# The MLP's second product by one level of Strassen's algorithm, a quarter of the 4096 features at a time, with tokens as rows, then turned back

## The chip, the cores and the metric

The kernel runs on one core of a Trainium2 chip. The core has five engines that work side by side, each through its own queue in order: TensorE (PE in the rows; its weight loads are shown apart as PEld), VectorE (DVE), ScalarE (ACT), GpSimd (POOL) and SyncE (SP), which issues the DMA transfers. They wait for each other through semaphores. SBUF is the on-chip memory of 128 partitions, PSUM the memory that TensorE writes its results to. The metric is the device time of one execution in microseconds (us), the median of three.

## The reference, cut to what matters

Two layers over 512 tokens of 1024 values each. The token mixers (attention, an RWKV-7 scan, a short convolution) stay as they are. The change is about the last line of a layer:

```python
for l in range(2):
    ...                                       # mixers, gates, x = x + merged @ w_out[l]
    h2 = rms_norm(x, mlp_norm[l])             # (1, 512, 1024)
    x = x + jnp.square(jax.nn.relu(h2 @ w_up[l])) @ w_down[l]   # up: 1024x4096, down: 4096x1024
```

`rms_norm(x, g) = x * rsqrt(mean(x*x) + 1e-6) * g`, a factor for each token and a gain for each of the 1024 values.

## The kernel before

**Number format.** All is float32, and every product is made as three TensorE products of a shorter type (`F32R`). Each operand is split into an upper part `hi` (the value cast to `F32R`) and a lower part `lo` (value minus `hi`). A product is then `hi*hi + hi*lo + lo*hi`: the three `mm` of `gemm_steps` (L283, L285, L287). A weight block of 128x512 is loaded to a `raw` tile by SyncE (L245), ScalarE casts it to `hi` (L246), VectorE subtracts for `lo` (L247); there are 4 buffers for `raw` and 4 for `hi` and `lo`. `split` and `split_into` do the same for activations.

**Layout.** The residual `xt` (tile `am`) has features on partitions: 8 tiles of 128 features x 512 tokens. An output tile of a product, 128 features x 512 tokens, is one bank of PSUM; it takes 8 blocks of 128 input features times 3, so 24 matmuls of 128x512, with the weights as the stationary operand and the activations moving.

**The MLP** (L1232 to L1259) goes through the 4096 inner features in four quarters `q`. In a quarter, 8 tiles of the first product are made from `h2`; ScalarE rectifies each out of PSUM (L1245), VectorE multiplies it by its PSUM tile, which squares it (L1246), and `split_into` makes the parts `us`. Then come 8 tiles of the second product, of 8 blocks of `us` each; VectorE multiplies each by the norm's factor (L1254, `rstd2`, the square of the token's factor spread over 128 partitions) and adds it to the residual (L1256). In the fourth quarter each tile goes out by DMA (L1259), in layer 0 to `x_spill`, in layer 1 to the output. PSUM tiles take turns over the tags g, a, b, c with two buffers each.

The norm's gain is in `h2` (`norm_in`). Its factor is not: `norm_scale` squares `xt` on ScalarE (L363) and sums over tiles on VectorE (L368); TensorE sums over partitions; the factor per token is then spread over all partitions by `spread`:

```python
pb = pt(pst)
for b in range(NB):
    e = tl("tok", (P, 4, C)).rearrange("p a b -> p (a b)")[:, 0:P]
    V.tensor_copy(e, rs[:, b:b + 1].to_broadcast([P, P]))
    nc.tensor.transpose(pb[:, b * P:(b + 1) * P], e, ident)
A.copy(dst, pb)
```

**What sets the order.** TensorE's instructions stand in the order in which the program is written. Those of the other engines are put in order at build time by the scheduler of the tile framework, by its own estimates of when operands are ready; a DMA is issued in that order too. A tile of a tag waits until the reader of the buffer's last content is done.

## Time and profile before

| | |
|---|---|
| median of 3 runs | 1600.34 us (1600.29 to 1600.41) |
| profiled execution, whole time | 1599.76 us |
| its span (first to last instruction) | 1598.0 us |
| TensorE busy | 1586.9 us |
| VectorE busy | 1026.8 us |
| ScalarE busy | 662.8 us |
| granted clock of TensorE | 1.00 |

"Busy" is the time in which an engine has an instruction under way. Neighbouring matmuls overlap, so the time of one is read from the distance of two starts. A row of the timeline gives start, duration, engine, line, operation, what is written from what is read, and how many equal ones are merged; in square brackets stands how long the engine was idle before, and what ended that.

### The profile page before, as it was taken

To read this page: it belongs to the slowest core of one execution; us is meant where nothing else is said; L and a number is where in the kernel's file an instruction comes from. 1 tells how busy PE (TensorE), PEld (TensorE's weight loads), DVE (VectorE), ACT (ScalarE), POOL (GpSimd) and SP (SyncE) were. 2 spreads that over 40 slices of the span, in tenths; PEclk is the share of its full clock that TensorE was granted. 3 is DMA by queue.
4 is the path that set the end of the run, shared out by engine and by line. 5 is a ranking of instruction groups with operands and counts; after the bars stand their busy time and mean duration, and the time that the engine had idled before them with its cause. 6 is when DMAs were issued, how large, how long until landed. Compare 5 with 4: busy or idle time off the path is not lost.

```text
span 1598.0 us, 22465 instructions
## 1 busy us (share of the span) xinstructions
PE 1586.9 (99%) x8046; PEld 1292.3 (81%) x8046; DVE 1026.8 (64%) x2035; ACT 662.8 (41%) x1470; POOL 184.9 (12%) x192
## 2 busy tenths in 40 slices
PE   9999999999999999999999999999999999999998
PEld 7888778877888888888877887888778888888887
DVE  8889677687654454444568986686886554444453
ACT  5433565454443332324334334655544423333241
POOL 1312015112000000000022221241130000000000
PEclk9999999999999999999999999999999999999999
DMA  5323322214323333333433242222143333333332
GB/s 178 106 70 119 107 61 80 76 54 163 102 93 98 96 98 99 94 98 99 140 91 86 86 132 90 61 73 73 54 165 106 93 93 99 99 94 98 99 94 97
DMA packets 84639, 156.25 MB, mean 98 GB/s; under 512 B 10032, under 2 KB 12080, under 8 KB 84016
## 3 DMA queue, kind: packets, MB, share of 16 engines
q1 hardware_dynamic: 84528, 154.83, 32.0%
q8 instruction: 63, 1.03, 0.3%
q14 instruction: 48, 0.39, 0.1%
HBM read 145.87 MB, written 8.91 MB: 97 GB/s over the span
## 4 chain that ended last, share of the span: by engine, by line
PE 98%; DVE 1%; DMA 0%; ACT 0%; issue 0%; SPq 0%; DVEq 0%
PE pg L283 16%; PE pg L285 16%; PE pg L287 16%; PE pb L283 4%; PE pb L287 4%; PE pb L285 4%; PE pa L287 4%; PE pc L287 4%; PE pc L283 4%; PE pa L283 4%; PE pa L285 4%; PE pc L285 4%; PE pa L1160 2%; PE pc L1186 1%; PE pb L1174 1%; PE pa L968 1%
## 5 line engine op out<-in xcount | busy, mean ns | idle before, releaser
L246 ACT CAST hi<-raw 128x512 fp32r<-128x512 f32 (+1 forms) x494 | 304.0, 618 | 592.2 <-PE pg L285 243.7
L247 DVE TENSOR_TENSOR lo<-raw,hi 128x512 fp32r<-128x512 f32 (+1 forms) x494 | 358.7, 727 | 239.9 <-ACT hi L246 235.0
L285 PE MATMUL pg<-xg,hi 128*128 128x512 f32 x736 | 296.8, 403 | 0.0
L283 PE MATMUL pg<-xg,hi 128*128 128x512 f32 x736 | 295.2, 401 | 0.7 <-DVE z L600 0.7
L287 PE MATMUL pg<-xg,lo 128*128 128x512 f32 x736 | 290.7, 395 | 0.0
L283 PEld LDWEIGHTS pg<-xg,hi 128*128 128x128 f32 x736 | 138.3, 188 | 33.5 <-issue 3.0
L287 PEld LDWEIGHTS pg<-xg,lo 128*128 128x128 f32 x736 | 138.4, 188 | 31.2 <-issue 3.4
L285 PEld LDWEIGHTS pg<-xg,hi 128*128 128x128 f32 x736 | 138.4, 188 | 30.8 <-issue 3.4
L330 POOL TENSOR_TENSOR t<-t,mhalf 128x4 f32<-128x4 f32 (+1 forms) x26 | 46.7, 1797 | 563.2 <-DVE t L341 535.0
L283 PE MATMUL pb<-xg,hi 128*128 128x512 f32 x144 | 56.4, 392 | 0.0
L287 PE MATMUL pb<-xg,lo 128*128 128x512 f32 x144 | 56.1, 389 | 0.0
L285 PE MATMUL pb<-xg,hi 128*128 128x512 f32 x144 | 56.1, 389 | 0.0
L1164 ACT ACTIVATE inv<-pa,t 128x128 f32<-128x128 f32 (+3 forms) x64 | 33.7, 527 | 47.7 <-DVE t L1162 44.9
L283 PE MATMUL pg<-mix,hi 128*128 128x512 f32 x128 | 51.4, 402 | 0.0
L287 PE MATMUL pg<-mix,lo 128*128 128x512 f32 x128 | 50.2, 393 | 0.0
L287 PE MATMUL pa<-xg,lo 128*128 128x512 f32 x128 | 50.0, 391 | 0.0
L283 PE MATMUL pc<-xg,hi 128*128 128x512 f32 x128 | 50.0, 390 | 0.0
L285 PE MATMUL pa<-xg,hi 128*128 128x512 f32 x128 | 49.8, 389 | 0.0
L287 PE MATMUL pc<-xg,lo 128*128 128x512 f32 x128 | 49.8, 389 | 0.0
L283 PE MATMUL pa<-xg,hi 128*128 128x512 f32 x128 | 49.8, 389 | 0.0
L285 PE MATMUL pc<-xg,hi 128*128 128x512 f32 x128 | 49.8, 389 | 0.0
L285 PE MATMUL pg<-mix,hi 128*128 128x512 f32 x112 | 44.5, 397 | 0.0
(453 smaller groups left out, 3353.4 us busy)
## 6 DMA issues: line engine op xcount, KB each, us to landing
raw<-in_w_dram SPq DMA_DIRECT2D x492, 256.0 KB, 2.6
z_spill<-z SPq DMA_DIRECT2D x16, 256.0 KB, 3.2
inv<-z_spill SPq DMA_DIRECT2D x16, 256.0 KB, 5.5
raw<-in_wq_dram SPq DMA_DIRECT2D x12, 192.0 KB, 2.4
am<-in_x_dram SPq DMA_DIRECT2D x8, 256.0 KB, 4.9
raw<-in_wkv_dram SPq DMA_DIRECT2D x8, 256.0 KB, 2.6
am<-in_x_dram SPq DMA_DIRECT2D x2, 1024.0 KB, 6.3
x_spill<-am SPq DMA_DIRECT2D x8, 256.0 KB, 2.8
```

Of the source, the lines that this page charges most:

```text
L246: A.copy(hi[:, c], raw[:, c])
L247: V.tensor_tensor(out=lo[:, c], in0=raw[:, c], in1=hi[:, c], op=ALU.subtract)
L283: mm(dst, hi[:, c0:c0 + P], ah, start=(k == 0), stop=False)
L285: mm(dst, hi[:, c0:c0 + P], al, start=False, stop=False)
L287: mm(dst, lo[:, c0:c0 + P], ah, start=False, stop=(k == n - 1))
L330: G.tensor_tensor(out=y, in0=v, in1=mhalf.to_broadcast([P, n]), op=ALU.pow)
L968: mm(pu[rr, hs], Zf[h // 2][rr, (h % 2) * 4 + b], R_[rr, hs], start=True, stop=True)
L1160: mm(psc[:, 0:n], qT[hf][h // 2][0:HD, h % 2, b * P:n], kT[hf][h // 2][0:HD, h % 2, 0:n], start=True, stop=True)
L1164: A.activation(out=pe[:, 0:n], in_=psc[:, 0:n], func=AF.Exp, bias=nm[:, h:h + 1], accum_out=rsum[:, h:h + 1])
L1174: nc.tensor.transpose(pq[:, kb * P:(kb + 1) * P], pe[:, kb * P:(kb + 1) * P], ident)
L1186: mm(po[halves[i], f], Vm[hf][kb // 2][:, kb % 2, 2 * f + i], pT[2 * f + i][:, kb * P:(kb + 1) * P], start=(kb == 0), stop=(kb == b))
```

## The change

The second product of a quarter, 512 tokens x 1024 features times 1024 features x 1024 outputs, is cut into halves along all three: A11, A12, A21, A22 are 256 tokens x 512 features, the weights' quarters 512 features x 512 outputs. One level of Strassen's algorithm (Winograd's form) makes it from 7 products of the halves instead of 8, with sums of activations (`S1` to `S4`) and of weights before them and sums of the results behind them. Each of the 7 is 2 token tiles of 128 tokens x 512 outputs, each of 4 blocks times 3, so 24 matmuls of 128x512. Activations are the stationary operand now and weights the moving one, so the results have tokens on partitions ("token-major").

- The sums of activations (L1311 to L1315 of the changed kernel) are made on VectorE on halves of 256 columns; the square is ScalarE's.
- Of the 16 weight blocks of a quarter, 12 are loaded during the first product into tiles that the mixers used before (`room`: `wa`, `wb`, `wc`, `wd`) and stay there; the last four are loaded into `wd` while S3 runs. The sums of weights are VectorE subtractions in place (L1324, L1325, and `less`, L1359). `split_block` makes `hi` and `lo` of each block as it is needed; the 4 buffers of `hi` and `lo` are the ones that the first product uses.
- A product's PSUM tiles (`px` with tag g, `pz` with a, `yp` with b) go on from one product to the next, and are added into the token-major sums `ya` (tag `mg`) by `add_out`, times the token's factor `r2` as a scalar per partition. The first product has tag c for itself, two buffers.
- In the last quarter `finish` turns 4 tiles of 128x128 back on TensorE, adds them to the residual and sends this part out, in rows of 512 bytes.
- `spread` is no longer called for this norm. For layer 1 the eight feature tiles of `xt` are used in the order 4 to 7, 0 to 3 (`K_ORDER`).

```diff
+K_ORDER = [tuple(range(KD)), (4, 5, 6, 7, 0, 1, 2, 3)]
+UP_ORDER = (0, 4, 1, 5, 2, 6, 3, 7)
+DOWN_ORDER = ((0, 0), (0, 1), (1, 1), (1, 0))
...
+    def split_block(src):
+        hi = tl("hi", (P, WW), F32R, bufs=BUFS["hl"])
+        lo = tl("lo", (P, WW), F32R, bufs=BUFS["hl"])
+        A.copy(hi, src)
+        V.tensor_tensor(out=lo, in0=src, in1=hi, op=ALU.subtract)
+        return hi, lo
...
-        rstd2, h2_steps, h2_spread = norm_scale(xt, True)
+        h2_steps, h2_at = norm_scale(xt, pst="a")
...
+        ya = [[tl("mg") for _ in range(2)] for _ in range(NB)]
+        room = [tl("col", (P, T + 1))[:, 0:T] for _ in range(7)] + [tl("kql", (P, 520))[:, 0:T] for _ in range(4)]
+        room += [tl("ext", (P, T + 1), bufs=1)[:, 0:T], tl("z"), tl("z"), tl("rstd", bufs=1), tl("mg")]
+        wa, wb, wc, wd = (room[4 * i:4 * i + 4] for i in range(4))
+        yp = [pt("b") for _ in range(2)]
...
+        def add_out(pd, b, dh):
+            r_ = r2[:, b:b + 1]
+            if (b, dh) in seen:
+                V.scalar_tensor_tensor(out=ya[b][dh], in0=pd, scalar=r_, in1=ya[b][dh], op0=ALU.mult, op1=ALU.add)
+            else:
+                A.activation(out=ya[b][dh], in_=pd, func=AF.Copy, scale=r_)
+            seen.add((b, dh))
+
+        def finish(b, dh):
+            pf = pt("c", (P, 4, P))
+            for i in range(4):
+                nc.tensor.transpose(pf[:, i], ya[b][dh][:, i * P:(i + 1) * P], ident)
+            part = xt[:, 4 * dh:4 * dh + 4, b * P:(b + 1) * P]
+            V.tensor_tensor(out=part, in0=pf, in1=part, op=ALU.add)
+            dst = xd if l < NL - 1 else out
+            nc.sync.dma_start(out=dst.rearrange("p (k t) -> p k t", t=T)[:, 4 * dh:4 * dh + 4, b * P:(b + 1) * P], in_=part)
+
         for q in range(4):
...
+            for n_, m in enumerate(UP_ORDER):
+                pu = pt("c")
+                run(gemm_steps(pu, None, h2), h2_steps if (q, n_) == (0, 1) else None)
...
                 rl = tl("inv")
                 A.activation(out=rl, in_=pu, func=AF.Relu)
-                V.tensor_tensor(out=rl, in0=pu, in1=rl, op=ALU.mult)
-                us.append(places(m, "mg") if q % 2 else places(m, None))
-                split_into(us[m], rl)
-            for m in range(8):
-                pd = pt(ptags[pi % 4])
-                pi += 1
-                gemm(pd, None, us)
-                d_ = tl("inv")
-                V.tensor_tensor(out=d_, in0=pd, in1=rstd2, op=ALU.mult)
-                xm = xt[:, m]
-                V.tensor_tensor(out=xm, in0=xm, in1=d_, op=ALU.add)
-                if q == 3:
-                    dst = xd if l < NL - 1 else out
-                    nc.sync.dma_start(out=dst[:, m * T:(m + 1) * T], in_=xm)
+                A.activation(out=rl, in_=rl, func=AF.Square)
+                us[m] = rl
+                if m >= 4:
+                    j = m - 4
+                    ua, ub = us.pop(j), us.pop(m)
+                    split_into(act["A11", j], ua[:, H1])
+                    s12, s34 = tl("inv"), tl("inv")
+                    V.tensor_tensor(out=s12[:, H1], in0=ua[:, H2], in1=ub[:, H2], op=ALU.add)
+                    V.tensor_tensor(out=s12[:, H2], in0=s12[:, H1], in1=ua[:, H1], op=ALU.subtract)
+                    split_into(act["S1S2", j], s12)
+                    V.tensor_tensor(out=s34[:, H1], in0=ua[:, H1], in1=ua[:, H2], op=ALU.subtract)
+                    V.tensor_tensor(out=s34[:, H2], in0=ub[:, H1], in1=s12[:, H2], op=ALU.subtract)
+                    split_into(act["S3S4", j], s34)
+                    split_into(act["A12A22", j], ub)
+
+                if n_ < 6:
+                    for i in (2 * n_, 2 * n_ + 1):
+                        down_block(i, (wa + wb + wc)[i])
+                elif n_ == 6:
+                    for j in range(4):
+                        V.tensor_tensor(out=wd[j], in0=wc[j], in1=wb[j], op=ALU.subtract)
+                        V.tensor_tensor(out=wb[j], in0=wb[j], in1=wa[j], op=ALU.subtract)
...
+            px, pz = [pt("g") for _ in range(2)], [pt("a") for _ in range(2)]
+            def product(a, blocks, acc, start, outs, before=None, after=None, by_tokens=False):
+                ws = {}
+                for t, j in [(t, j) for t in range(2) for j in range(4)] if by_tokens else \
+                        [(t, j) for j in range(4) for t in range(2)]:
+                    if j not in ws:
+                        if before:
+                            before(j)
+                        ws[j] = split_block(blocks[j])
+                        if after:
+                            after(j)
...
+                    mm(acc[t], ah[:, c], hi, start=(start and j == 0), stop=False, skip_group_check=True)
+                    mm(acc[t], ah[:, c], lo, start=False, stop=False, skip_group_check=True)
+                    mm(acc[t], al[:, c], hi, start=False, stop=(j == 3), skip_group_check=True)
...
+            product("A11", wa, px, True, [(0, 0)])
+            product("S1", wb, pz, True, [(1, 1)])
+            product("S2", wb, px, False, [(0, 1)], before=less(wb, wc, wb))
+            product("S3", wd, px, False, [(1, 1)], after=lambda j: down_block(12 + j, wd[j]))
+            product("S4", wc, pz, False, [(0, 1)])
+            if last:
+                finish(2, 1)
+                finish(3, 1)
+            product("A12", wd, yp, q == 0, [(0, 0)] if last else [])
+            if last:
+                finish(0, 1)
+                finish(1, 1)
+            product("A22", wb, px, False, [(1, 0)], before=less(wb, wd, wb), by_tokens=last)
+        finish(2, 0)
+        finish(3, 0)
```

In this place on TensorE the program goes from the last block of S2 to the first of S3, in the second quarter of layer 0. `pg_6116` and `pg_6117` are `px[0]` and `px[1]`; `hi` and `lo` are parts of a weight block, `ar` and `mix` of activations.

```order
L1344 MATMUL pg_6116<-hi_6238,ar_4975 128x512
L1345 MATMUL pg_6116<-lo_6239,ar_4975 128x512
L1346 MATMUL pg_6116<-hi_6238,ar_4975 128x512
L1344 MATMUL pg_6117<-hi_6238,ar_4975 128x512
L1345 MATMUL pg_6117<-lo_6239,ar_4975 128x512
L1346 MATMUL pg_6117<-hi_6238,ar_4975 128x512
L1344 MATMUL pg_6116<-hi_6250,mix_4958 128x512
L1345 MATMUL pg_6116<-lo_6251,mix_4958 128x512
```

The first matmul of S3 writes the tile that S2 has just finished, so `add_out` has to read it out in between; before, a product of 24 matmuls had the other buffer of its tag, and then three more tags, to go on in.

This is VectorE's queue at the same place: L248 makes the lower part of a block of weights, L1359 and `col`, `kql`, `ext`, `z` are blocks of weights and their differences, L1277 is `add_out`.

```order
L1359 TENSOR_TENSOR kql_4994<-ext_4998,kql_4994 128x512
L1277 SCALAR_TENSOR_TENSOR mg_4984<-pa_6118,r_0_5149,mg_4984 128x512
L1277 SCALAR_TENSOR_TENSOR mg_4986<-pa_6119,r_0_5149,mg_4986 128x512
L248 TENSOR_TENSOR lo_6228<-col_4993,hi_6227 128x512
L248 TENSOR_TENSOR lo_6239<-kql_4994,hi_6238 128x512
L248 TENSOR_TENSOR lo_6251<-z_4999,hi_6250 128x512
L248 TENSOR_TENSOR lo_6262<-z_5000,hi_6261 128x512
L1277 SCALAR_TENSOR_TENSOR mg_4980<-pg_6116,r_0_5149,mg_4980 128x512
L248 TENSOR_TENSOR lo_6273<-rstd_5001,hi_6272 128x512
L1277 SCALAR_TENSOR_TENSOR mg_4982<-pg_6117,r_0_5149,mg_4982 128x512
L1359 TENSOR_TENSOR col_4991<-z_4999,col_4991 128x512
L248 TENSOR_TENSOR lo_6284<-mg_5002,hi_6283 128x512
```

The two additions from `px` stand with one lower part between them, behind four lower parts of S2 and S3; from the first sum of activations of the last up tile (L1311) to the second of these additions there are 28 rows in VectorE's queue.

And this is VectorE at the end of layer 0, before and then after; L311 and L326 are the norm's lower parts for layer 1, L247 and L262 lower parts of loaded weights, L368 and L384 sums of squares, L1288 adds turned tiles to the residual.

```order
L1254 TENSOR_TENSOR inv_7665<-pc_7628,rstd_4955 128x512
L247 TENSOR_TENSOR lo_7792<-raw_7790,hi_7791 128x512
L1256 TENSOR_TENSOR am_4586<-am_4586,inv_7665 128x512
L368 TENSOR_TENSOR inv_7705<-inv_7701,inv_7703 128x512
L368 TENSOR_TENSOR inv_7709<-inv_7705,inv_7707 128x512
L311 SCALAR_TENSOR_TENSOR xg_7698<-am_4586,pp_82,xg_7697 128x512
```

```order
L1277 SCALAR_TENSOR_TENSOR mg_4983<-pg_7524,r_0_5149,mg_4983 128x512
L1288 TENSOR_TENSOR am_4586<-pc_7849,am_4586 128x4x128
L326 SCALAR_TENSOR_TENSOR xg_7891<-am_4586,pp_82,xg_7890 128x512
L1288 TENSOR_TENSOR am_4586<-pc_7856,am_4586 128x4x128
L384 TENSOR_TENSOR inv_7927<-inv_7923,inv_7925 128x512
L326 SCALAR_TENSOR_TENSOR xg_7895<-am_4586,pp_82,xg_7894 128x512
L262 TENSOR_TENSOR lo_7959<-raw_7957,hi_7958 128x512
L384 TENSOR_TENSOR inv_7931<-inv_7927,inv_7929 128x512
L1277 SCALAR_TENSOR_TENSOR mg_4985<-pg_7525,r_0_5149,mg_4985 128x512
```

Between the last two additions from `px`, on which the last two calls of `finish` wait, seven other operations stand now.

## Rows read from the trace of the kernel before

**Rows 1.** The page of the profile: the span, the engines' busy time, TensorE's granted clock in 40 slices (tenths of full speed), and the shares of the chain of work that ended last, by engine.

```profile
span 1598.0 us, 22465 instructions
PE 1586.9 (99%) x8046; PEld 1292.3 (81%) x8046; DVE 1026.8 (64%) x2035; ACT 662.8 (41%) x1470; POOL 184.9 (12%) x192
...
PEclk9999999999999999999999999999999999999999
...
PE 98%; DVE 1%; DMA 0%; ACT 0%; issue 0%; SPq 0%; DVEq 0%
```

**Rows 2.** Busy time of each engine in three stretches of the MLP of layer 0; behind the engines the granted clock, the DMA engines' share and GB/s.

```profile
508.00:549.00 41.00, 41.00 (x182) 33.97 (x181) 18.90 (x29) 10.61 (x18) 0.00 (x0) 1.00 0.33 98
549.00:590.00 41.00, 41.00 (x182) 33.95 (x181) 20.65 (x31) 17.36 (x30) 0.00 (x0) 1.00 0.35 99
590.00:631.00 41.00, 41.00 (x182) 33.95 (x182) 19.00 (x30) 9.58 (x17) 0.00 (x0) 1.00 0.33 97
```

**Rows 3.** The timeline of TensorE in the MLP of layer 0: the first matmul of one tile and the first of the next, with 23 left out between.

```profile
472.42 0.39 PE L283 MATMUL pg<-xg,hi 128*128 128x512 f32 x1
...
477.86 0.39 PE L283 MATMUL pa<-xg,hi 128*128 128x512 f32 x1
```

**Rows 4.** The timeline of TensorE where `spread` stands in the MLP of layer 0 (L350), and the two matmuls behind it.

```profile
466.05 0.38 PE L350 MATMUL pc<-ident,tok 128*128 128x128 f32 x2
466.64 0.47 PE L350 MATMUL pc<-ident,tok 128*128 128x128 f32 x2 [0.21 <-DVE tok L349]
466.87 0.47 PE L283 MATMUL pc<-xg,hi 128*128 128x512 f32 x1
467.18 0.39 PE L285 MATMUL pc<-xg,hi 128*128 128x512 f32 x1
```

**Rows 5.** The timeline of TensorE in the attention part: four transposes of 128x128, merged, and the two matmuls behind them.

```profile
374.04 0.60 PE L1174 MATMUL pb<-ident,inv 128*128 128x128 f32 x4
374.39 0.48 PE L285 MATMUL pg<-xg,hi 128*128 128x512 f32 x1
374.71 0.39 PE L287 MATMUL pg<-xg,lo 128*128 128x512 f32 x1
```

**Rows 6.** The timeline of TensorE in the attention part: first and last of 8 matmuls with weights as the stationary operand, then first and last of 21 with activations as the stationary operand.

```profile
212.96 0.40 PE L285 MATMUL pg<-xg,hi 128*128 128x512 f32 x1
...
214.58 0.39 PE L287 MATMUL pg<-xg,lo 128*128 128x512 f32 x1
...
218.19 0.39 PE L1053 MATMUL pa<-prep,prep 128*128 128x512 f32 x1
...
222.84 0.40 PE L1055 MATMUL pb<-prep,col 128*128 128x512 f32 x1
```

**Rows 7.** Groups of instructions by line and form: count, busy time, mean ns of one, idle time before. The first two are of the stretch 467 to 816 us, the others of the whole span (VectorE's, then ScalarE's).

```profile
L247 DVE TENSOR_TENSOR lo<-raw,hi 128x512 fp32r<-128x512 f32 x129 | 89.0, 690 | 96.8 <-ACT hi L246 95.3
L246 ACT CAST hi<-raw 128x512 fp32r<-128x512 f32 x128 | 79.5, 621 | 190.5 <-PE pc L285 47.2 <-PE pa L285 44.5 <-PE pg L285 44.0
...
L1229 DVE SCALAR_TENSOR_TENSOR am<-pg,am 128x512 f32<-128x512 f32 x16 | 11.1, 692 | 23.8 <-PE pg L287 23.8
...
L911 DVE TENSOR_TENSOR yb<-yb,t 128x256 f32<-128x256 f32 x8 | 3.4, 420 | 0.1
...
L363 ACT ACTIVATE inv<-am 128x512 f32<-128x512 f32 x32 | 19.0, 619 | 0.0
```

**Rows 8.** The timeline of VectorE: three operations in a row of which none reads what another wrote.

```profile
829.53 0.68 DVE L545 TENSOR_TENSOR col<-pa,rstd 128x512 f32<-128x512 f32 x1
830.13 0.68 DVE L545 TENSOR_TENSOR col<-pb,rstd 128x512 f32<-128x512 f32 x1
830.73 0.68 DVE L545 TENSOR_TENSOR col<-pg,rstd 128x512 f32<-128x512 f32 x1
```

**Rows 9.** The timeline of ScalarE: a cast of weights and the rectification behind it.

```profile
548.59 0.62 ACT L246 CAST hi<-raw 128x512 fp32r<-128x512 f32 x1 [2.10 <-PE pa L285]
549.12 0.59 ACT L1245 ACTIVATE inv<-pa 128x512 f32<-128x512 f32 x1
```

**Rows 10.** The timeline of all engines at the kernel's end, from the last matmul to the last store.

```profile
1592.98 0.39 PE L287 MATMUL pc<-mg,lo 128*128 128x512 f32 x1
1593.41 0.69 DVE L1254 TENSOR_TENSOR inv<-pc,rstd 128x512 f32<-128x512 f32 x1 [4.02 <-PE pc L287]
1594.13 0.69 DVE L1256 TENSOR_TENSOR am<-am,inv 128x512 f32<-128x512 f32 x1
1594.85 0.33 SPq L1259 DMA_DIRECT2D out_dram<-am  x1
```

**Rows 11.** Transfers, from four views: a step of the chain that ended last (from the reader that frees the buffer to the first use), two rows of the issues by line (count, KB each, median us to landing), SyncE's own queue at 377 us, and the engines, clock, DMA share and GB/s from 380 to 390 us.

```profile
192.52 2.76 DMA raw<-in_wkv_dram
...
raw<-in_w_dram SPq DMA_DIRECT2D x492, 256.0 KB, 2.6
...
inv<-z_spill SPq DMA_DIRECT2D x16, 256.0 KB, 5.5
...
377.67 0.33 SPq L245 DMA_DIRECT2D raw<-in_w_dram  x1
378.04 2.33 SPq L1213 DMA_DIRECT2D inv<-z_spill  x5
...
380.00:390.00 10.00, 10.00 (x68) 8.17 (x67) 5.17 (x11) 3.99 (x8) 3.31 (x3) 1.00 0.89 318
```

More of the change, by code (lines that the diff above doesn't have):

```diff
@@ L351, in spread, with norm_in, norm_scale @@
         A.copy(dst, pb)
-    def norm_in(xt, gcol):
-        return [split("xg", xt[:, k], gcol[:, k:k + 1]) for k in range(KD)]
-    def norm_scale(xt, squared, behind=None):
+    def norm_in(xt, gcol, order=range(KD)):
+        parts = {k: split("xg", xt[:, k], gcol[:, k:k + 1]) for k in order}
+        return [parts[k] for k in range(KD)]
+    def norm_scale(xt, behind=None, order=range(KD), pst="c"):
         acc = None
-        for k in range(KD):
+        for k in order:
             s = tl("inv")
@@ new lines, in trunk @@
+        places_ = [tl("mix", (P, T), F32R) for _ in range(8)] + [tl("prep", (P, T), F32R) for _ in range(10)]
+        for _ in range(4):
+            both = tl("ar", (P, 2, T), F32R)
+            places_ += [both[:, 0], both[:, 1]]
+        places_ += [tl("mg", (P, T), F32R) for _ in range(2)]
+        H1, H2 = slice(0, 256), slice(256, T)
+        act = {}
+        for j in range(4):
+            p_ = places_[7 * j:7 * j + 7]
+            act["A11", j] = (p_[0][:, H1], p_[0][:, H2])
+            for i, (n1, n2) in enumerate((("S1", "S2"), ("S3", "S4"), ("A12", "A22"))):
+                h_, l_ = p_[1 + 2 * i], p_[2 + 2 * i]
+                act[n1, j], act[n2, j] = (h_[:, H1], l_[:, H1]), (h_[:, H2], l_[:, H2])
+                act[n1 + n2, j] = (h_, l_)
@@ new lines, in trunk, with down_block @@
+        ya = [[tl("mg") for _ in range(2)] for _ in range(NB)]
[3 more added lines that the diff above has]
+        yp = [pt("b") for _ in range(2)]
+        seen = set()
+        def down_block(i, dst):
+            n = sum(sizes[:first + 16 + i]) * P
+            nc.sync.dma_start(out=dst, in_=w[n:n + WW * P].rearrange("(p n) -> p n", p=P))
@@ new lines, in product @@
+            def product(a, blocks, acc, start, outs, before=None, after=None, by_tokens=False):
[8 more added lines that the diff above has]
+                            after(j)
+                    hi, lo = ws[j]
+                    ah, al = act[a, j]
+                    c = slice(t * P, (t + 1) * P)
+                    mm(acc[t], ah[:, c], hi, start=(start and j == 0), stop=False, skip_group_check=True)
+                    mm(acc[t], ah[:, c], lo, start=False, stop=False, skip_group_check=True)
+                    mm(acc[t], al[:, c], hi, start=False, stop=(j == 3), skip_group_check=True)
+                    if by_tokens and j == 3:
+                        for th, dh in outs:
+                            add_out(acc[t], 2 * th + t, dh)
+                        if t == 0:
+                            finish(0, 0)
+                            finish(1, 0)
+                if not by_tokens:
+                    for t in range(2):
+                        for th, dh in outs:
+                            add_out(acc[t], 2 * th + t, dh)
@@ new lines, in less @@
+            def less(dst, a_, b_):
+                return lambda j: V.tensor_tensor(out=dst[j], in0=a_[j], in1=b_[j], op=ALU.subtract)
+            last = q == 3
+            product("A11", wa, px, True, [(0, 0)])
[6 more added lines that the diff above has]
+                finish(3, 1)
```

53 lines of the change are left out of this document (24 added, 29 removed).

## The prediction

> **What bounds the kernel now.** I read the page first: TensorE is busy for 1586.9 of 1598.0 us, VectorE 64%, ScalarE 41%; the clock row reads 9 in every slice, and the chain that ended last is 98% TensorE [rows 1]. A kernel with such a page gets faster only by what leaves TensorE's queue, as long as nothing that is put on the other engines makes TensorE wait. The table by stages says the same of the two MLPs: 41.00 of 41.00 us busy, VectorE near 19 to 21 us of 41, ScalarE 10 to 17, clock 1.00 [rows 2]. Next I took the price of a product from its pace, not from its "busy" of 0.39 us, since neighbours overlap: 24 matmuls of 128x512 start between 472.42 and 477.86, so one costs 0.2267 us and an output tile of 24 costs 5.44 us [rows 3].
>
> **What leaves TensorE.** Before, a quarter of the second product is 8 tiles of 24, so 192 matmuls; after, it is 7 products of 24, so 168. That is 24 fewer in each of 4 quarters of 2 layers: 192 x 0.2267 = **43.5 us less**. The spread of the norm's factor over all rows goes too (the factor now rides as a scalar per token): in its place in the trace the next matmul starts at 466.87 instead of 466.05, and the one after 0.31 us later instead of 0.23 [rows 4], so 0.9 us a layer, **1.8 us less**.
>
> **What comes to TensorE.** Sixteen calls of `finish`, four 128x128 transposes each. Four transposes of this kind stand at 374.04; the matmul behind starts 0.35 later, and the next one 0.32 after that instead of 0.23 [rows 5], so four cost 0.44 us and the sixteen **7.0 us more**. The Trainium skill (TensorE: Matmul & The Clock Gate, Part 4: PE-mode transpose) gives about 275 ns for a single 128x128 transpose inside a kernel. By it the 64 would cost 17.6 us and the sum below would be 10.6 us worse; the trace has four in 0.44 and does not agree.
>
> The products have the same shape but other roles: activations stationary, weights moving. The nearest row is a product of this form in the attention part: 20 starts from 218.19 to 222.84, 0.2325 us each; its neighbours in the old roles run 7 starts from 212.96 to 214.58, 0.2314 each [rows 6]. So most of the slower pace belongs to that stretch, and 0.0011 to the roles. Bounds for 1344 such matmuls: 0 and 1344 x 0.0058 = 7.8 us; I take 1344 x 0.0011 = **1.5 us**, since [rows 3] are of the MLP and it is the quieter stretch.
>
> **What VectorE and ScalarE get.** In the first half of a quarter (8 tiles, 43.5 us) and the second (168 matmuls, 38.1 us), an operation of 512 columns takes 0.69 us on VectorE and 0.62 on ScalarE, a multiply-add out of PSUM 0.69, 256 columns 0.42 [rows 7]. VectorE starts one that does not depend on the last 0.60 us after it, not 0.69 [rows 8], and ScalarE 0.53 [rows 9]. Second half on VectorE: 28 lower parts of weights, 8 differences, 12 additions into `ya`: 48 x 0.605 = 29.0 of 38.1 us. First half: 16 lower parts, 12 of activations, 8 differences, 20 pieces of 256 columns at 0.335 (0.42 less the same overlap): 28.5 of 43.5 us. ScalarE has 28 x 0.53 = 15 us in the second half, and less than 30 in the first; its square is a function that the kernel runs already, at 0.62 [rows 7]. Neither is the bound on average, so what counts is a place where VectorE's queue is late.
>
> **The late place.** Take t = 0 where product A11 starts. ScalarE casts the last block of it, then rectifies (0.53 later) and squares (0.63 later) the last up tile, 0.62 us, so VectorE can begin on that tile at t = 1.8. From there 28 rows stand without a pause in its order, L1311 to the second addition from `px`: 4 of 256 columns, 24 of 512. TensorE wants:
> - the lower part of S1's fourth block at 5.44 + 3 x 1.36 + 0.23 = 9.75. Fourteen rows stand ahead (4 x 0.335 + 10 x 0.605 = 7.4), so it starts at 9.2 and is there at 9.9: 0.15 late;
> - S2's third at 14.0; 21 rows ahead, there at 14.15: 0.15 late;
> - `px[0]` read out when S3 begins, 16.3 + 0.3: its addition starts when S2's last matmul into it is through (16.3 - 4 x 0.23 + 0.3 late + 0.43 to see it [rows 10] = 16.1) and is done by 16.85: 0.25 late;
> - `px[1]` 0.68 later: its addition is two rows on, done at 18.1: 0.55 late.
>
> That is 1.1 us for a quarter. The first quarter of a layer has none of it (its first sums go to ScalarE by copies); I leave 0.2. At the end of layer 0 the last addition from `px` stands behind eight more rows, of which seven belong to norms, splits and turned tiles: started when the first token tile is done they take about 8 x 0.62 = 5.0, then 0.7 for the addition, against 4.0 us of TensorE's second tile and three calls of `finish`: 1.8 late. In layer 1 nothing stands between: 0.5 (0.43 to see the last matmul, 0.69, less the third `finish`, 0.44, and what overlaps). Waits: 6 x 1.1 + 2 x 0.2 + 1.8 + 0.5 = **9.3 us more**.
>
> **Loads.** The kept blocks (`wd`, then `wc`, `wb`) are loaded into their places when their last split has read them, and VectorE's order has subtractions that wait for these loads (L1359 after S3's blocks). From the end of a reader to the first use of a loaded block the chain has 2.76 us; the median of the weight loads is 2.6 [rows 11]. With 2.76 the three subtractions of S3 wait 0.2, 0.3 and 0.9 us on VectorE and the blocks behind still come in time: 0. SyncE issues one in 0.33 to 0.47 us [rows 11], and some eight in eleven us are 2 MB, 190 GB/s; the trace has carried 318 [rows 11].
>
> **The tail.** Before: 1592.98 (last matmul) to 1598.0, 5.0 us, with two VectorE operations and the store [rows 10]. After: the wait and the four transposes are counted above; behind them stand 0.2 us of transposes still running, one VectorE operation and the same store of 3.1 us, 4.1 us after TensorE's last slot against 4.8 before: **0.7 us less**. Its rows of 512 instead of 2048 bytes I price between 0 and 1 us and take 0.
>
> **The sum**, against the profiled execution of 1599.8 us (1598.0 and 1.8 around it): -43.5 - 1.8 + 7.0 + 1.5 + 9.3 - 0.7 = -28.2, so 1571.6. The median of the runs shown lies 0.6 above that execution, so I forecast **1572 us**, 1.8% less. With the low bounds (pace 0, waits of half the size) it is 1566, with the high one for the pace 1578.
>
> **Rivals.**
> 1. VectorE has no overlap in this mix. [rows 8] speaks against it; for it, that 28 operations with waits on three other engines are not the three starts shown there. With 0.69 and 0.42 a step, the 28 rows end at 1.8 + 4 x 0.42 + 24 x 0.69 = 20.0 instead of 17.7, so 3.4 us late a quarter instead of 1.1; six quarters give 14 us more: **1586**. The Trainium skill (VectorE: DVE Perf Modes, The DRAIN you can't avoid) says that an operation starts only when the one before has left the pipe; that is this rival, and the trace, where starts lie 0.60 apart at 0.69 each [rows 8], does not agree.
> 2. Slower than before: the loads land late, and VectorE waits in order for them. In the burst of reloads at 378 the median landing is 5.5 us [rows 11]. The loads in S3 hang one behind the other (split, load, subtraction, split), so each us past about 3 costs about 2 us a quarter: at 5.5 it is 5 more in eight quarters, 38 us: 1610. It breaks even where a quarter waits 4.6 us, at a landing of 5 us. Against it: that burst was eight loads in five us with the DMA engines at 0.89; here four stand in five to six us.
> 3. The pace of [rows 6] is that of the roles: 6.3 us more, **1578**.
> 4. Nothing of VectorE's queue shows, and the pace is that of [rows 3]: 1562.
>
> **Chances.** The forecast with waits of 5 to 16 us (1566 to 1579) 0.58; rival 1 and other ways to lose 10 to 20 us in VectorE's queue (1580 to 1592) 0.2; rival 3 0.08; rival 4 (below 1566) 0.06; rival 2 0.08, of which 0.05 slower, 0.02 about even and 0.01 still faster. From 0.2% (3.2 us) on the runs, which lie within 0.12 us, tell a change. So faster 0.93, same 0.02, slower 0.05. The range for 8 in 10 leaves out rival 2 and most of rival 4: 1565 to 1590.
>
> **What would show it.** In the changed kernel's trace: 0.227 to 0.228 between matmuls in products A11 to A22; idle of TensorE of 1 to 2 us a quarter, nearly all at S3's first two tiles, ended by the additions from `px` (L1277), and about 2 us at the end of layer 0; VectorE busy without a pause over the 28 rows; loads of the kept blocks landing in 2.6 to 3 us. I would be wrong if the waits fall on the lower parts (L248) in A12 and A22, behind L1359 that wait for loads (rival 2), if VectorE's starts lie 0.69 apart (rival 1), or if ScalarE's queue, where a cast can wait for a buffer of TensorE's ahead of a rectification, makes an up tile wait, which I take as hidden by the second buffer of `pc`: uncovered it would cost up to 1.2 us a tile, 77 us in all.

## The result and the profile after

The changed kernel takes **1579.36 us** (median of four runs, 1578.26 to 1579.9) against 1600.32 in the same series: a ratio of 0.9869 (95% interval 0.9857 to 0.988), 21 us less. The forecast was 1572 in a range of 1565 to 1590: the sign and the place of the gain were right, 7 us of it did not come. The profiled execution has a span of 1577.6 us, 20.4 less than before. All times here are medians of runs at a granted clock of 0.99 to 1.00; one run of the three edits together (below), at 0.85, took 1721.79 us and is left out.

The page of the changed kernel: span, busy time, the chain that ended last, and one kind of the loads of kept blocks (count, KB, median us to landing).

```profile
span 1577.6 us, 22682 instructions
PE 1559.8 (99%) x7910; PEld 1259.6 (80%) x7910; DVE 1179.4 (75%) x2351; ACT 797.2 (51%) x1708; POOL 182.2 (12%) x192
...
PE 91%; DVE 5%; DMA 2%; ACT 1%; issue 0%; SPq 0%; DVEq 0%
...
col<-in_w_dram SPq DMA_DIRECT2D x56, 256.0 KB, 2.7
```

Against [rows 1], TensorE has 136 instructions fewer (192 matmuls and 8 transposes of `spread` gone, 64 transposes come), VectorE is 153 us busier and ScalarE 134. The chain is no longer all TensorE: 5% of it runs through VectorE and 2% through a transfer. Those shares say where to look; a cut by stage says how much. The matmul that sums the squares over partitions stands once in each mixer part and once in each MLP, so its four places cut the program in the same way before and after. TensorE's rows of it, of the kernel before:

```profile
28.13 0.28 PE L336 MATMUL pc<-ones,inv 128*128 128x1 f32 x2
...
454.67 0.28 PE L336 MATMUL pc<-ones,inv 128*128 128x1 f32 x2
...
820.58 0.16 PE L336 MATMUL pc<-ones,inv 128*128 128x1 f32 x1
...
1249.06 0.28 PE L336 MATMUL pc<-ones,inv 128*128 128x1 f32 x2
```

and of the changed kernel:

```profile
28.64 0.28 PE L351 MATMUL pc<-ones,inv 128*128 128x1 f32 x2
...
456.39 0.16 PE L351 MATMUL pa<-ones,inv 128*128 128x1 f32 x1
...
810.89 0.16 PE L351 MATMUL pc<-ones,inv 128*128 128x1 f32 x1
...
1242.10 0.28 PE L351 MATMUL pa<-ones,inv 128*128 128x1 f32 x2
```

| stretch | before | after | difference |
|---|---|---|---|
| start to the first sum | 28.13 | 28.64 | +0.5 |
| rest of layer 0's mixers | 426.54 | 427.75 | +1.2 |
| MLP of layer 0, start of layer 1 | 365.91 | 354.50 | -11.4 |
| rest of layer 1's mixers | 428.48 | 431.21 | +2.7 |
| MLP of layer 1 to the end | 348.94 | 335.50 | -13.4 |

The two MLPs give 24.8 us; the mixers, in which TensorE's work is the same as before, take 4.4 of it back. The prediction had no term for them.

**Inside the MLP** the waits stand where the prediction put them. TensorE's timeline in the second quarter of layer 0: S1's fourth block, then the end of S2 and the first two tiles of S3.

```profile
586.53 0.39 PE L1344 MATMUL pa<-hi,ar 128*128 128x512 f32 x1
587.02 0.50 PE L1345 MATMUL pa<-lo,ar 128*128 128x512 f32 x1
587.37 0.40 PE L1346 MATMUL pa<-hi,ar 128*128 128x512 f32 x1
...
593.79 0.40 PE L1346 MATMUL pg<-hi,ar 128*128 128x512 f32 x1
594.42 0.47 PE L1344 MATMUL pg<-hi,mix 128*128 128x512 f32 x1 [0.24 <-DVE mg L1277]
594.73 0.39 PE L1345 MATMUL pg<-lo,mix 128*128 128x512 f32 x1
...
595.59 0.50 PE L1344 MATMUL pg<-hi,mix 128*128 128x512 f32 x1 [0.24 <-DVE mg L1277]
595.93 0.39 PE L1345 MATMUL pg<-lo,mix 128*128 128x512 f32 x1
```

Starts should lie 0.227 apart. S1's fourth block loses 0.26 where it waits and 0.12 at the start behind, S2's third block (not shown) 0.07 and 0.11; S3's tiles lose 0.40 + 0.08 and 0.41 + 0.11. The brackets show 0.24, since a matmul's modelled end runs into the pause: the distance of starts is the price, not the bracket. VectorE at the same place, from the first of the 28 rows to the additions out of `px`:

```profile
578.80 0.42 DVE L1311 TENSOR_TENSOR inv<-inv,inv 128x256 f32<-128x256 f32 x1 [0.47 <-ACT inv L1304]
...
587.49 0.69 DVE L1359 TENSOR_TENSOR col<-kql,col 128x512 f32<-128x512 f32 x1
588.09 0.69 DVE L248 TENSOR_TENSOR lo<-col,hi 128x512 fp32r<-128x512 f32 x1
...
593.53 0.75 DVE L1277 SCALAR_TENSOR_TENSOR mg<-pg,r,mg 128x512 f32<-128x512 f32 x1 [0.42 <-PE pg L1346]
594.19 0.68 DVE L248 TENSOR_TENSOR lo<-rstd,hi 128x512 fp32r<-128x512 f32 x1
594.79 0.74 DVE L1277 SCALAR_TENSOR_TENSOR mg<-pg,r,mg 128x512 f32<-128x512 f32 x1
```

Starts are 0.60 apart in the mix too. And VectorE is idle for 0.42 us before the first addition, waiting for TensorE: by then it is not late any more.

**At the end of layer 0** the two additions stand 5 us apart on VectorE, with seven rows between, and the `finish` behind the second waits 1.77 us (the prediction: 1.8):

```profile
782.80 0.75 DVE L1277 SCALAR_TENSOR_TENSOR mg<-pg,r,mg 128x512 f32<-128x512 f32 x1 [0.48 <-PE pg L1346]
...
787.79 0.74 DVE L1277 SCALAR_TENSOR_TENSOR mg<-pg,r,mg 128x512 f32<-128x512 f32 x1
...
788.59 0.66 PE L1286 MATMUL pc<-ident,mg 128*128 128x128 f32 x4 [1.77 <-DVE mg L1277]
```

**In the mixers of layer 1** the changed kernel's timeline shows what is new: among the last gate merges, VectorE has a weight subtraction of the first quarter (L1324) that waits for its load, a merge (L618) stands behind it, and TensorE behind that; 3.5 us later a cast is late too.

```profile
1169.20 6.76 DMA col<-in_w_dram
...
1175.98 0.69 DVE L1324 TENSOR_TENSOR rstd<-kql,col 128x512 f32<-128x512 f32 x1 [1.50 <-DMA col<-in_w_dram]
...
1177.33 0.50 PE L298 MATMUL pg<-prep,hi 128*128 128x512 f32 x1 [0.76 <-DVE inv L618]
```

The first line is from the chain that ended last: that load took 6.76 us in the burst of z_spill reloads, against 2.7 for its kind. The cast that is late stands at 1180.92, behind 0.57 us of idle time.

How full VectorE is there, the kernel before shows: from 392 to 406 us it is busy for 14.00 of 14.00 us. A merged tile is 12 matmuls, 2.72 us of TensorE, and three rows of VectorE, a merge (L607), a split (L325, not shown) and a lower part of weights (L247). GpSimd adds up the tile just merged (1.60 us), and the VectorE row that starts during this addition takes 1.77 us in place of 0.68 and ends 0.55 behind it. So the three rows take 2.90:

```profile
392.04 0.67 DVE L607 SCALAR_TENSOR_TENSOR inv<-inv,pg 128x512 f32<-128x512 f32 x1
...
392.86 1.61 POOL L1217 TENSOR_TENSOR mg<-mg,inv 128x512 f32<-128x512 f32 x1 [1.29 <-DVE inv L607]
...
393.24 1.77 DVE L247 TENSOR_TENSOR lo<-raw,hi 128x512 fp32r<-128x512 f32 x1
...
394.94 0.68 DVE L607 SCALAR_TENSOR_TENSOR inv<-inv,pg 128x512 f32<-128x512 f32 x1
```

Before, VectorE falls back by 0.18 us a tile there, and TensorE's distances stay at 0.227: the lag doesn't reach TensorE before the merges end. In the changed kernel VectorE comes late to these tiles, and TensorE takes its pace, in layer 0 for six tiles, 1.1 of the 1.2 us. The first matmuls of two of them lie 2.89 apart:

```profile
398.11 0.47 PE L298 MATMUL pg<-prep,hi 128*128 128x512 f32 x1
...
401.00 0.47 PE L298 MATMUL pg<-prep,hi 128*128 128x512 f32 x1
```

### The profile page after: what moved, and what is told of

Same layout as the page of the kernel before. It is cut to its first block, busy times and chain, and to the rows that moved or that the text cites. A ratio compares the mean times of both kernels' runs of the same rounds, so it can differ in the third digit from the quotient of the medians.

```text
span 1577.6 us, 22682 instructions
## 1 busy us (share of the span) xinstructions
PE 1559.8 (99%) x7910; PEld 1259.6 (80%) x7910; DVE 1179.4 (75%) x2351; ACT 797.2 (51%) x1708; POOL 182.2 (12%) x192
## 4 chain that ended last, share of the span: by engine, by line
PE 91%; DVE 5%; DMA 2%; ACT 1%; issue 0%; SPq 0%; DVEq 0%
PE pg L298 12%; PE pg L300 12%; PE pg L302 12%; PE pc L300 7%; PE pc L298 7%; PE pc L302 7%; PE pg L1344 3%; PE pg L1345 3%; PE pg L1346 3%; PE pa L1171 2%; PE pa L1345 1%; PE pa L1346 1%; PE pa L1344 1%; DVE mg L1277 1%; DVE lo L248 1%; PE pc L1197 1%
## 5 line engine op out<-in xcount | busy, mean ns | idle before, releaser
L261 ACT CAST hi<-raw 128x512 fp32r<-128x512 f32 (+1 forms) x366 | 224.6, 618 | 332.7 <-PE pg L300 150.0
L262 DVE TENSOR_TENSOR lo<-raw,hi 128x512 fp32r<-128x512 f32 (+1 forms) x366 | 264.7, 725 | 123.9 <-ACT hi L261 122.0
L300 PE MATMUL pg<-xg,hi 128*128 128x512 f32 x608 | 246.9, 406 | 0.0
L298 PE MATMUL pg<-xg,hi 128*128 128x512 f32 x608 | 245.4, 404 | 0.7 <-DVE z L611 0.7
L302 PE MATMUL pg<-xg,lo 128*128 128x512 f32 x608 | 241.0, 396 | 0.0
L302 PE MATMUL pc<-xg,lo 128*128 128x512 f32 x512 | 199.4, 389 | 0.0
L300 PE MATMUL pc<-xg,hi 128*128 128x512 f32 x512 | 199.2, 389 | 0.0
L298 PE MATMUL pc<-xg,hi 128*128 128x512 f32 x512 | 199.2, 389 | 0.0
L300 PEld LDWEIGHTS pc<-xg,hi 128*128 128x128 f32 x512 | 96.1, 188 | 20.1
L298 PEld LDWEIGHTS pc<-xg,hi 128*128 128x128 f32 x512 | 96.1, 188 | 20.0
L302 PEld LDWEIGHTS pc<-xg,lo 128*128 128x128 f32 x512 | 96.1, 188 | 19.8
L247 ACT CAST hi<-col 128x512 fp32r<-128x512 f32 x104 | 64.6, 621 | 78.9 <-PE pc L300 30.8
L248 DVE TENSOR_TENSOR lo<-col,hi 128x512 fp32r<-128x512 f32 x104 | 71.4, 688 | 34.2 <-ACT hi L247 33.7
L247 ACT CAST hi<-kql 128x512 fp32r<-128x512 f32 x48 | 29.8, 622 | 34.3 <-PE pg L1346 24.9
```

The source lines that it names most:

```text
L247: A.copy(hi, src)
L248: V.tensor_tensor(out=lo, in0=src, in1=hi, op=ALU.subtract)
L261: A.copy(hi[:, c], raw[:, c])
L262: V.tensor_tensor(out=lo[:, c], in0=raw[:, c], in1=hi[:, c], op=ALU.subtract)
L298: mm(dst, hi[:, c0:c0 + P], ah, start=(k == 0), stop=False)
L300: mm(dst, hi[:, c0:c0 + P], al, start=False, stop=False)
```

## The experiments

All edits are to the changed kernel (1579.4 us). The theory after the result: besides the waits inside the MLP, which the forecast named and sized a little small, the loss is the first quarter's eight subtractions in VectorE's queue among the gate merges. The first rival: it is the transfers themselves, which delay other loads. The second: VectorE as a whole has too little room, so that a wait taken away at one place comes back at the next.

**The subtractions of the first quarter held until the MLP**

```diff
+                    with tc.issue_after(r2_ins.ins) if q == 0 else nullcontext():
                         for j in range(4):
                             V.tensor_tensor(out=wd[j], in0=wc[j], in1=wb[j], op=ALU.subtract)
                             V.tensor_tensor(out=wb[j], in0=wb[j], in1=wa[j], op=ALU.subtract)
```

> The eight weight subtractions (L1324, L1325) of the first quarter of each layer are held in VectorE's queue behind the square of the token's factor, so that they run inside the MLP; their loads stay where they are. Theory: in the changed kernel these eight rows stand in VectorE's queue among the last gate merges (380 to 406 us and 1165 to 1195 us), and the lower parts of weights behind them came late; TensorE loses 1.1 us there in layer 0 and 2.7 us in layer 1. With them held, the two losses go and the time is 1575.6 us (1575.0 to 1576.4); no idle row of TensorE stands between 1170 and 1190. Rival: the transfers are to blame, since the loads of kept blocks come in the burst of z_spill reloads (one landed in 6.76 us); they are not moved here, so the raw weights would still be late and the time stays at 1579.4 (1578.5 to 1580).

1575.3 us (1575.25 to 1575.67), ratio 0.9845 (0.9831 to 0.986). The four rows of the cut:

```profile
28.47 0.28 PE L351 MATMUL pc<-ones,inv 128*128 128x1 f32 x2
...
454.89 0.28 PE L351 MATMUL pa<-ones,inv 128*128 128x1 f32 x2
...
809.25 0.28 PE L351 MATMUL pc<-ones,inv 128*128 128x1 f32 x2
...
1237.80 0.28 PE L351 MATMUL pa<-ones,inv 128*128 128x1 f32 x2
```

The mixers are back at 426.4 and 428.6 (before: 426.5 and 428.5), the MLPs unchanged. The loads were not moved, and the one of the burst is as late as it was (6.57 us): with no row of VectorE's queue waiting for it, it costs nothing that shows. How the loss divides can be read from the eight profiled executions that keep these rows in place (the changed kernel's and seven below, two layers each). Where no subtraction waits for the load, the mixers lose 1.0 to 1.3 us, as in layer 0 above (there VectorE also waits 0.98 us at a subtraction into `z`, until GpSimd has read that tile). Where one waits, by 0.15 to 2.27 us, the loss is 1.2 us and the wait on top, within 0.2 in all sixteen stretches: 2.7 us for a wait of 1.50 in layer 1 above, and 3.4 for the longest. So the rows by themselves cost 1.2 us a layer, and a late load costs what the row that needs it makes VectorE wait. That wait differs from execution to execution; without it the spread of the runs shrinks here from 1.6 us to 0.4.

**S4 between S2 and S3**

```diff
             product("S2", wb, px, False, [(0, 1)], before=less(wb, wc, wb))
+            product("S4", wc, pz, False, [(0, 1)])
             product("S3", wd, px, False, [(1, 1)], after=lambda j: down_block(12 + j, wd[j]))
-            product("S4", wc, pz, False, [(0, 1)])
...
```

> Product S4 (PSUM tag a) is put between S2 and S3 (both PSUM tag g), and the calls of finish follow their sums; nothing else. Theory: S3's first two tiles wait for the additions that read px out (0.99 us in each of six quarters, 0.37 in the first of each layer), and with 24 matmuls between, the additions are done long before: 6.7 us less, 1572.7 (1571.5 to 1574). Rival: VectorE's queue is late by itself, and the same lateness is met at the lower parts of the next product, or at A12, whose blocks are loaded only while S3 runs, 5.4 us ahead (landing 2.7, cast 0.62, lower part 0.69): about 1 us a quarter comes back, 1578 to 1580.

1572.47 us (1571.9 to 1573.65), ratio 0.9828 (0.9814 to 0.9843): 6.9 us less, as the theory said. TensorE goes from S4's last matmul to S3's first without a pause:

```profile
598.93 0.39 PE L1346 MATMUL pa<-hi,ar 128*128 128x512 f32 x1
599.16 0.39 PE L1344 MATMUL pg<-hi,mix 128*128 128x512 f32 x1
```

The waits at S1's fourth and S2's third block stay as they were, and none to speak of appears at A12 (one of 0.11 in the last quarter of layer 0), although its blocks are now loaded only one product ahead; a new one of 0.60 stands at A22's fourth block at the end of layer 0. The Trainium skill (Perfetto Trace Analysis, Optimizing Tensor Performance: Matmuls) says that groups of matmuls should take turns over PSUM banks, so that one is read out while the next is made; the original order breaks that at one place a quarter, and this run agrees.

**The last addition of layer 0 ahead of the next layer's norm** (`hold` is the last `add_out` of layer 0; the split of the first tile is left as it is):

```diff
-        parts = {k: split("xg", xt[:, k], gcol[:, k:k + 1]) for k in order}
+        for i, k in enumerate(order):
+            with tc.issue_after(hold.ins) if hold and i else nullcontext():
+                parts[k] = split("xg", xt[:, k], gcol[:, k:k + 1])
...
+                with tc.issue_after(hold.ins) if hold else nullcontext():
+                    V.tensor_tensor(out=n_, in0=acc, in1=s, op=ALU.add)
```

> At the end of layer 0 the norm's sums (L384) and the lower parts of the norm behind the first (L326) are held behind the last addition out of px; five rows stand between the last two additions then, not seven. Theory: TensorE's idle time of 1.77 us before the last finish but one is VectorE's queue, 0.60 us a row; two rows fewer give 1.2 us: 0.55 us idle there, 1578.2. Rival: the held rows are needed at once in layer 1, and what is gained is lost at the first lower parts of layer 1: 1579.4, with new idle time behind 790 us.

1578.37 us (1577.49 to 1579.45), ratio 0.9862 (0.9846 to 0.9879). The runs of both kernels spread by more than the 1.0 us between their medians, so the time alone doesn't decide; the trace does:

```profile
789.08 0.66 PE L1293 MATMUL pc<-ident,mg 128*128 128x128 f32 x4 [0.50 <-DVE mg L1284]
```

0.50 us idle in place of 1.77, with no new idle time behind it: two rows of VectorE's queue, 0.6 us each.

**The three together**

> The three edits together. If each wait is a place of its own the gains add: 1579.4 - 3.8 - 6.7 - 1.2 = 1567.7 (1566.5 to 1570). If VectorE's queue as a whole is the limit, they overlap: 1572 or more.

1568.1 us (1567.6 to 1568.4), ratio 0.98 (0.9783 to 0.9816). The gains add (1567.7 expected): three places, not one shortage. The second rival falls here, but for the 0.6 us at A22 that came with S4's new place.

**Two rows of VectorE's queue taken away**: A11's additions left out in quarters 1 to 3.

```diff
-            product("A11", wa, px, True, [(0, 0)])
+            product("A11", wa, px, True, [(0, 0)] if q == 0 else [])
```

> The two additions of product A11 into the token-major sums are left out in quarters 1 to 3 (a part of the result is missing): two rows fewer among the 28 of VectorE's queue, 1.3 us. If TensorE's wait at S3 is VectorE's queue being late, all waits of a quarter go (0.38 at S1's fourth block, 0.18 at S2's third, 0.99 at S3): 6 x 1.55 = 9.3 us, 1570. If the wait at S3 is the way itself (the last matmul into px 0.43 us to be seen, an addition of 0.75, a lower part between the two), only the first two go: 6 x 0.56 = 3.4 us, 1576.0, and S3's first two tiles still start with idle time ended by L1277.

1575.12 us (1574.7 to 1575.96), ratio 0.9843 (0.9825 to 0.9861): nearer to the second reading. The pauses at S1 and S2 are gone (no two starts there lie more than 0.24 us apart in quarters 1 to 3), S3's is as before:

```profile
593.44 0.47 PE L1344 MATMUL pg<-hi,mix 128*128 128x512 f32 x1 [0.26 <-DVE mg L1277]
```

So there are two kinds of wait in a quarter: 0.56 us at S1 and S2 is VectorE's queue being late, 1.0 at S3 is the way from the last matmul through the addition, which two rows fewer in the queue do not shorten and a different order hides. What a shorter addition or no lower part between the two additions would give was not tried.

**The queue's part too**: the three edits of before, and the casts and lower parts of the last block of S3/S4 and A12/A22 behind S2's third and fourth block.

```diff
+            def held(j):
+                if j >= 2:
+                    with tc.issue_after(last_lo[0].ins):
+                        split_into(*later.pop(0))
...
-            product("S2", wb, px, False, [(0, 1)], before=less(wb, wc, wb))
+            product("S2", wb, px, False, [(0, 1)], before=less(wb, wc, wb), after=held)
```

> The three edits of e134_all, and the lower parts and casts of S3/S4's and A12/A22's last block, which S1 and S2 don't read, are held in the queues until S2's third and fourth block are split. Theory: the waits at S1's fourth block (0.38) and S2's third (0.18) are VectorE's queue; two rows (1.2 us) fewer stand ahead of both, more than the 0.3 that VectorE is late, so both go in six quarters: 1568.3 - 3.4 = 1564.9 (1564 to 1566). Rival: the queue is only reordered, and S2's fourth or S4's first block is late by as much: 1568.

**1564.14 us** (1563.54 to 1564.2), ratio 0.9772 (0.9756 to 0.9788), the fastest here: 15.2 us less than the changed kernel. In its trace no two starts of a product lie more than 0.24 us apart in the first three quarters of either layer, but for the place of the sum of squares; what is left of idle time in the MLPs stands at the two layers' ends (0.73 and 0.41 before the last `finish`, and 0.49 by starts at A22's fourth block in layer 0). Its span is 1562.1 us.

**Later loads**, twice: the four loads during S3 as two each, of every other piece of 128 bytes, and then of 64.

```diff
+            dst, src = (t_.rearrange("p (a b n) -> p b a n", b=2, n=32) for t_ in (dst, src))
+            for b in range(2):
+                nc.sync.dma_start(out=dst[:, b], in_=src[:, b])
```

> The four loads of kept blocks that are issued while S3 runs are each made as two loads of every other 128-byte piece, so that they take longer; everything else is as in the changed kernel. It puts the prediction's rival 2 to the test: there, loads that land later than about 3 us stop VectorE's queue, because its subtractions (L1359) wait for them in order, at about 2 us a quarter for each us: with a landing of 4 us 1579.4 + 9 = 1588, of 5 us 1604, of 6 us 1631. If a late landing is hidden by the work that stands between, 1579.4 to 1581 whatever the landing.

> As f1_slow_loads, with pieces of 64 bytes, so that the four loads during S3 land later still. With pieces of 128 bytes they landed in 4.0 us and cost 1.6 us in all, since VectorE's wait for them (2.5 us in one quarter) was nearly all hidden. Theory: the cover is used up there, and from here each further us costs about 2 us in each of the eight quarters: landing of 5 us 1597, of 6 us 1613, of 8 us 1645. Rival: the loads run side by side and the cover is as long as a product (5.4 us), so that up to a landing of some 6 us hardly anything is lost: below 1590.

With 128 bytes 1580.96 us (1580.64 to 1581.27), ratio 0.988 (0.9859 to 0.9901); with 64 bytes 1616.46 (1615.5 to 1617.41), 1.01 (1.008 to 1.012), slower than before. The issues of both (median to landing), for 128 bytes VectorE's longest wait in the second quarter, and for 64 bytes the wait there (the last of three) behind which TensorE pauses:

```profile
z<-in_w_dram SPq DMA_DIRECT2D x32, 128.0 KB, 3.5
...
599.14 0.69 DVE L1365 TENSOR_TENSOR col<-z,col 128x512 f32<-128x512 f32 x1 [1.96 <-DMA z<-in_w_dram]
```

```profile
z<-in_w_dram SPq DMA_DIRECT2D x32, 128.0 KB, 4.9
...
608.93 0.69 DVE L1365 TENSOR_TENSOR col<-rstd,col 128x512 f32<-128x512 f32 x1 [1.85 <-DMA rstd<-in_w_dram]
...
610.94 0.68 PE L1351 MATMUL pa<-lo,prep 128*128 128x512 f32 x1 [2.15 <-DVE lo L248]
```

Both expectations were too simple. At a landing of 3.5 us (4.0 in the quarter shown) VectorE waits 2.5 us for loads, and TensorE loses almost nothing of it: the lower parts that it needs next were already made. At 4.9 the cover is gone: 37 us lost, 4.6 a quarter, of which some is not waiting at all but the matmuls behind the pause, 0.43 apart at a granted clock of 0.51 (611.0 to 614.4 us). The prediction's rival 2 is right in its mechanism, but it put a steady price from 3 us on and the break-even at 5; the two runs lose 1.6 us against the changed kernel at 3.5, and at 4.9 they stand 16 us above the kernel before.

**`finish` without TensorE**

```diff
-            pf = pt("c", (P, 4, P))
-            for i in range(4):
-                nc.tensor.transpose(pf[:, i], ya[b][dh][:, i * P:(i + 1) * P], ident)
+            pf = ya[b][dh].rearrange("p (k t) -> p k t", t=P)
```

> finish without TensorE: the token-major sums are added to the residual as they are, not turned back (that part of the computation is left out). Theory: 64 transposes in 16 calls cost 0.44 us a call, 7.0 us; the wait of 1.8 us at the end of layer 0 goes with them, since layer 1's first product no longer stands behind the last additions, and the tail loses the way through TensorE, 0.8 us: 1579.4 - 9.6 = 1569.8 (1569 to 1571.5). Rival, by the price that the Trainium skill gives for one transpose alone: 17.6 us for the 64, and 1559.

1576.36 us (1575.83 to 1577.03), ratio 0.9852 (0.9835 to 0.9867): 3.0 us less, not 9.6. The run doesn't isolate the transposes: without their wait VectorE's order changed, and in layer 0 lower parts of A22's third and fourth block now stand behind other work, 0.8 and 2.3 us late, with the matmuls behind the longer pause 0.43 apart for 3.2 us, at a granted clock of 0.50 (the bracket names a MEMSET of the same moment; what the matmul reads is the lower part `lo<-kql`, made from 784.47 to 785.15):

```profile
785.21 0.79 PE L1343 MATMUL pg<-lo,mg 128*128 128x512 f32 x1 [2.11 <-DVE col L553]
```

The price of a call is read better from the changed kernel itself: eight transposes at 1568.18, and the next product 0.79 us later, with 0.08 more at its second start, so 0.43 a call, as [rows 5] gave. The Trainium skill (TensorE: Matmul & The Clock Gate, Part 4: PE-mode transpose) has about 275 ns for one, in bf16. The trace agrees as to how long one lasts, 0.27 us here, but the eight start 0.11 apart: eight of them take 1.03 us in the row below, and the next product starts after 0.79. The prediction, and the rival of this run, took that length for the price of one, and so arrived at 17.6 us.

```profile
1568.18 1.03 PE L1286 MATMUL pc<-ident,mg 128*128 128x128 f32 x8
...
1568.97 0.47 PE L1344 MATMUL pg<-hi,mix 128*128 128x512 f32 x1
```

**`K_ORDER` undone**: `K_ORDER = [tuple(range(KD)), tuple(range(KD))]`.

> K_ORDER undone: layer 1 takes the feature tiles in their natural order, so its first product needs tile 0, which the last calls of finish complete. Theory: the first matmul of layer 1 then waits for the last addition to the residual, a cast on ScalarE (0.73) and a lower part on VectorE (0.74), but the sums of squares no longer stand ahead of the last addition out of px: 0.5 to 1.5 us more in all, 1580.3 (1579 to 1582). Rival: the order is worth a full chain of split and addition for each of four tiles: 3 us or more, over 1582.

1583.64 us (1581.34 to 1584.16), ratio 0.9894 (0.9879 to 0.991): 4.3 us more, the rival's side. The pause was as expected, 0.41 before the last `finish` and 2.50 behind it, 1.1 more than 1.77. What was not expected is the row below it: after that pause TensorE runs at a granted clock of 0.50 for 6 us, and 13 distances of starts from 790.52 to 796.59 take 6.1 us and not 3.0. That is the other 3.1. In the row of the stretch the last three figures are granted clock, DMA share and GB/s.

```profile
790.52 0.79 PE L567 MATMUL pg<-xg,hi 128*128 128x512 f32 x1 [2.50 <-ACT xg L325]
...
790.50:796.50 6.00, 5.98 (x13) 4.41 (x14) 5.71 (x9) 6.00 (x11) 0.00 (x0) 0.50 0.40 131
```

## Why the prediction was right, and where 7 us went

| term | forecast | measured |
|---|---|---|
| 192 matmuls fewer, `spread` | -45.3 | as counted, by 136 instructions fewer |
| 16 calls of `finish` | +7.0 | 0.43 a call, +7.0 |
| pace with the roles changed | +1.5 | +1.0, behind the waits; the roles 0 |
| waits in six quarters | +6.6 | 1.57 to 1.61 each, +9.5 |
| in the first quarters | +0.4 | 0.37 each, +0.7 |
| end of layer 0, end of layer 1 | +2.3 | by starts 1.99 and 0.57 (brackets 1.77 and 0.41), +2.6 |
| tail | -0.7 | -0.4 |
| everything ahead of the MLPs | 0 | +4.4 |
| sum | -28.2 | -20.5 (span: -20.4) |

- **The gain** came as counted. The pace was that of the MLP's own rows: 24 starts of S4, from 600.49 to 605.92, lie 0.2263 apart. Over all 1272 undisturbed distances the mean is 0.2275, which is 1.0 us in all, but that is not the roles: 0.9 of it lies in the first 16 starts behind a wait, and where a quarter has no wait (the fastest kernel above, 575.45 to 613.31) 167 distances have a mean of 0.2267. So rival 3 falls: the slower pace of [rows 6] belonged to the stretch.

```profile
600.49 0.39 PE L1344 MATMUL pa<-hi,mix 128*128 128x512 f32 x1
...
605.92 0.39 PE L1344 MATMUL pb<-hi,mix 128*128 128x512 f32 x1
```

- **The waits** were at the four places that "The late place" named. Its sizes were small by 0.5 us a quarter: four waits, which by themselves came to 1.16 where 1.1 was forecast, and each slows the start behind it as well, by 0.07 to 0.12. [rows 4, 5] show that (0.31 in place of 0.23), and it was used for the transposes but not for the waits. A third of the waits stands at S1 and S2, where "What would show it" had nearly all at S3.
- **Rival 1** falls: in the 28 rows VectorE's starts lie 0.60 apart at 0.69 each, as in [rows 8]. The rule of the Trainium skill (VectorE: DVE Perf Modes, The DRAIN you can't avoid) that an operation starts when the pipe is empty would have them 0.69 apart. The same section lets an operation that is not held back start earlier, which the prediction left out; with that the rows agree.
- **The step that failed** is the one on what VectorE gets. It counted "8 differences" in the first half of every quarter. For the first quarter of a layer they don't stand in the MLP: the scheduler took their tiles to be free and their loads to come early, and put them among the gate merges of the mixers, where VectorE was full (14.00 of 14.00 us, 2.90 a tile against TensorE's 2.72) and its rows had no price in the sum. 3.9 of the 4.4 us are the mixers', 1.2 a layer for the rows and 1.50 for the wait for a load, and they went when the rows were held. The remaining 0.5, at the program's start, was not followed up; in the profiled executions of the edited kernels it lies between 0.2 and 1.0.
- **The tail** kept 4.35 us behind TensorE's last slot (1572.81 + 0.44) and not 4.1: from the issue of the last store, 1574.22, to the end of the program it is 3.4 us, where [rows 10] had 3.2; its rows of 512 bytes had been priced between 0 and 1 us.

```profile
1572.81 0.66 PE L1286 MATMUL pc<-ident,mg 128*128 128x128 f32 x4 [0.41 <-DVE mg L1277]
...
1574.22 0.37 SPq L1290 DMA_DIRECT2D out_dram<-am  x1
```

## What to carry to other kernels

Where a change hands work to an engine that is 64% busy on average, ask for each new instruction in which stage it will be run, and read that stage's rows; what a scheduler takes to be ready is moved forward, into a stage that may be full, and an in-order engine then waits there for its load. Price a row by the rows of that stage (1.77 us where GpSimd adds, not 0.68). When two products in a row accumulate into the same PSUM tiles with a read between, put another product between them: here that was worth 1 us in six of eight quarters, which two rows fewer in VectorE's queue had not given. Price a wait at TensorE by the distance of starts, with the slower start behind it.

## What was not expected of the hardware

After some pauses TensorE came back at the lower of its two clock levels (1.2 of 2.4 GHz): after 2.11 us in the run without the turn, 2.50 in the one with the natural order, 2.15 and others in the one with the 64-byte loads, the matmuls behind stand 0.43 us apart for 3 to 6 us, at a granted clock of 0.50 to 0.51. After the 1.77 us at the end of layer 0 of the changed kernel they stand 0.23 apart. The length of the pause doesn't decide alone: in the run with the 64-byte loads the lower level followed a pause of 1.94 us (at 1413 us) and did not follow one of 2.03 (at 1326). The slow starts cost 1.6 us in the first case and 3.1 in the second, there more than the pause had grown (1.1). On the pages of these runs the clock row reads 9 in every slice; only the table of a narrow stretch shows it.

A VectorE row that starts while GpSimd makes one of its 1.60 us additions of the gate merges takes 1.77 to 1.79 us in place of 0.68, in both kernels.

The time of a load by the size of its pieces, at 256 KB for a block: 2.7 us in rows of 2048 bytes; as two loads of half the size 3.5 with pieces of 128 bytes and 4.9 with pieces of 64.
